# Moved SBUF homes, attention results stored as two parts, and another order of loads in a one-core encoder layer

## The chip, the core and the metric

The kernel runs on one core of one Trainium2 chip. The metric is device time in microseconds, the median of several runs of the same program; lower is better. The engines named here are PE (TensorE, matrix products), PEld (its weight loads), DVE (VectorE), ACT (ScalarE), POOL (GpSimd) and SP (SyncE, whose queue issues nearly all DMA transfers). SBUF is the on-chip memory of 128 partitions; PSUM holds the results of the matmuls. An address below is a byte offset within a partition.

## The reference

One layer over a sequence of 2048 tokens of width 1024, in float32. Two sub-layers follow each other; both take a normalised input that is scaled and shifted by values worked out from a conditioning vector c.

```
mod = silu(c) @ w_ada + b_ada                  # six vectors: shift, scale, gate, twice
h = rmsnorm(x, g1) * (1 + sc1) + sh1
q, k, v (two groups of 8 heads of 64) = split(h @ w_in)
o_sb = stick_breaking_attention(q_sb, k_sb, v_sb)              # strictly causal
o_ca = chunked_relpos_attention(rmsnorm(q_ca), rmsnorm(k_ca), v_ca, rel_bias)
x = x + gt1 * (concat(o_sb, o_ca) @ w_o)
h = rmsnorm(x, g2) * (1 + sc2) + sh2
x = x + gt2 * (square(relu(h @ w1)) @ w2)
```

Stick-breaking attention weighs key s for query t by sigmoid(z_ts) times the product of the (1 - sigmoid) of all keys between them. The other group is a softmax over the query's chunk of 64 and the eight chunks before it, with a learned bias for the distance.

## The kernel before

The host hands the sequence over reversed and transposed, so that tokens lie along the free dimension. They are cut into four blocks of TB = 512 (numbered g or tb, 0 to 3) and the width into KT = 8 slices of P = 128.

**Two parts for every operand.** A float32 matrix product is made as three fast products: each operand is split into a high part (rounded by a copy on ACT, L128) and a low part (the rest, by a subtraction on DVE or POOL, L129), and `mm3` (L186 onwards) adds high*high, high*low and low*high into one PSUM bank. A part tile has the shape [128, 2, 512]: high, then low, 4096 bytes a partition. In a matmul one operand is loaded first and stays (the weights, PEld) and the other is streamed past it (the moving operand).

**Three stages.** The first projects h onto q, k and v (tiles pq, pt) and also prepares w_o, stored to DRAM as parts in `scr_wo`, and the bias. Some of the projections of blocks 1 and 0 are left to the second stage. The second stage is the attention: for every head and block there are units (SB for the first group, CA for the second) of four steps each, 448 steps in all. A step makes scores (z, cz, ct), weights (sigmoid and a scan on DVE, or a softmax), and, eight steps later, transposes of the weights (wt, against the constant ident), their two parts (wth, wtl) and the products with the values (acc). Instructions of PE, ACT, DVE and POOL stand in program order here; SP's order is made by a scheduler at build time, with eight transfers in flight at most by its semaphores. Loads of q, k and v are issued two units ahead.

**Filler.** Between the steps PE gets other matmuls, a few at a time, from a list of generators: `fill_qkv` for block 1 (its moving operand ht1 is still in SBUF), `fill_qkv` for block 0 (moving operand fht, one load of 4 MB from `scr_h`), and `outproj(g)` for g = 3, 2, 1, the output projection of an attended block. `fill` hands out credit per step, so that the list ends about with the attention; after certain yields it rests for some steps (RESTS). What is left at the end is run by `drain`, and `outproj(1)` is: its rows 4 to 7 stand behind the last acc.

**Results of the attention.** `finish` puts the two halves of a head together on ACT and DVE; behind every second head, the [128, 512] float32 tile goes to `scr_m` (L592), 32 in all. `outproj` (L822) loads the eight of its block again as mo, and splits them into the tile mx on ACT and POOL, two before its first row and the rest within it. mx, fht and ht1 share one home, the pool hxp, of one buffer of 32 KB.

**Behind the attention** comes the third stage, in one list of steps. Eight steps `Mixed(0, n)` project block 0 (tile pso): step 0 loads and splits the eight tiles of scr_m (L1284 to L1286), and each step's w_o parts (wo) and row of x (xr) are loaded one step ahead, from L1290 on. `right_blocks(1, k)` (tiles ty, h), four calls at steps 2 to 5, load four tiles each of scr_x, scale them by POOL and ACT, combine and split them on DVE and ACT into the operands h of the MLP. The MLP makes its two products by a scheme of seven products in place of eight (Strassen's, in Winograd's form): `First` (ps<-h,opw, w1) and `Second` (ps<-oph,opv, w2), each for two halves mb of the sequence, 1344 matmuls a time.

A pool is a stretch of SBUF that is cut into a fixed number of equal buffers; pools are stacked, and a pool opened only to fill space (padn, pado, padp, padm) moves what is stacked on it. Homes in this program: h at 8192 + 4096 i, opw, oph and opv at 155456 + 4096 i, ident at 1152. The stack begins with 1024 bytes reserved for DMA descriptors.

Of the kernel before, what the change touches and what calls it, by code (L numbers as in the profile page):

```python
# [18 lines left out]
P = 128  # L19
# [3 lines left out]
NH = 8  # L23
# [44 lines left out]
def encoder_kernel(ctx, tc, xT, c, g1, g2, w_in, gqk, bias, w_o, w1, w2, w_ada, b_ada, out):  # L68
# [11 lines left out]
    hxp = hx.enter_context(tc.tile_pool(name="hxp", bufs=1))  # L80
# [7 lines left out]
    scr_m = scratch("scr_m", [P, TB], NTB, KT)  # L88
# [89 lines left out]
    def norm_apply(which, x, k, dst, pl, tg):  # L178

        j = 3 * which * KT + k  # L180
        a, b = aff[:, which, k : k + 1], mod[:, j : j + 1]
        hi, lo = dst[:, k, 0, :], dst[:, k, 1, :]
        act.activation(x, x, AF.Identity, scale=a, bias=b)
        split(hi, lo, x)
# [37 lines left out]
    with ExitStack() as ph:  # L222
# [3 lines left out]
        np_ = ph.enter_context(tc.tile_pool(name="np_", bufs=2))  # L226
        stp = ph.enter_context(tc.tile_pool(name="stp", bufs=4))
# [46 lines left out]
        def project(piece, tb, ht, wh, wl):  # L274
# [4 lines left out]
            if not ca and kind < 2:  # L279
                for n in range(2):  # L280
                    ps = pp.tile([P, TB], F32, tag="ps", name=f"pq{nm}_{n}")
                    cl = slice(n * P, (n + 1) * P)
                    for k in range(KT):
                        mm3(ps, wh[:, k, cl], wl[:, k, cl], ht[:, k, 0, :], ht[:, k, 1, :], k == 0, k == KT - 1)
# [5 lines left out]
            for t2 in range(2):  # L290
                ps = pp.tile([P, TB], F32, tag="ps", name=f"pt{nm}_{t2}")
                for tt in range(2):
                    tl = slice((2 * t2 + tt) * P, (2 * t2 + tt + 1) * P)
                    for k in range(KT):
                        mm3(
                            ps[:, tt * CW : (tt + 1) * CW], ht[:, k, 0, tl], ht[:, k, 1, tl],
# [96 lines left out]

        def h_tile(tb):
            if tb % 2:
                return hxp.tile([P, KT, 2, TB], F32R, tag="hx", name=f"ht{tb}")
            return hp.tile([P, KT, 2, TB], F32R, tag="hp", name=f"ht{tb}")
# [52 lines left out]
        for k in range(KT):  # L450
# [11 lines left out]
            for m, p in enumerate(first):  # L462
                hi, lo = (wh2[:, k], wl2[:, k]) if p == 2 else (wide[:, k, 0, p], wide[:, k, 1, p])
                for n in range(2):
                    cl = slice(n * P, (n + 1) * P)
                    mm3(
                        pss[2 * m + n], hi[:, cl], lo[:, cl], hts[3][:, k, 0, :], hts[3][:, k, 1, :],
# [29 lines left out]
        for n, (f, p, t) in enumerate(jobs):  # L497
# [18 lines left out]
            if (f, p, t) == (1, 6, 1):  # L516
                norms.flush()
                end_norm(0, h_tile(0))
                sp.dma_start(scr_h, hts[0].bitcast(F32))
# [16 lines left out]
    with ExitStack() as ph:  # L536
        kp0 = ph.enter_context(tc.tile_pool(name="kp0", bufs=3))
        owp = ph.enter_context(tc.tile_pool(name="owp", bufs=3))
        fp = ph.enter_context(tc.tile_pool(name="fp", bufs=3))
# [3 lines left out]
        pado.tile([P, 304], F32, tag="pad", name="pado")  # L543
        zw = ph.enter_context(tc.tile_pool(name="zw", bufs=12))
        wtp = ph.enter_context(tc.tile_pool(name="wtp", bufs=4))
        padp = ph.enter_context(tc.tile_pool(name="padp", bufs=1))
        zp = ph.enter_context(tc.tile_pool(name="zp", bufs=6))
        padp.tile([P, 656], F32, tag="pad", name="padp")
# [33 lines left out]
        def finish(u):  # L582
# [8 lines left out]
            if u.h % 2:  # L591
                sp.dma_start(scr_m[u.g, u.ca * 4 + u.h // 2], o)  # L592
# [182 lines left out]
        RESTS = {"pause": 3, "wait": 4, "next": 1, "start": 3}  # L775

        def fill_qkv(tb, ht, pieces):

            if ht is None:
                ht = hxp.tile([P, KT, 2, TB], F32R, tag="hx", name=f"fht{tb}")  # L780
                sp.dma_start(ht.bitcast(F32), scr_h)
# [8 lines left out]
            for n, piece in enumerate(pieces):  # L790
                grp, hf = divmod(piece, 2)
                w, nxt = nxt, []
                for j in range(2):
                    nm = f"f{tb}_{piece}_{j}"
                    ps = ppd.tile([P, TB], F32, tag="ps", name=f"p{nm}")
                    last = 0 if grp < 2 else 1
                    for tt in range(last + 1):
                        tl = slice((2 * j + tt) * P, (2 * j + tt + 1) * P)
                        for k in range(KT):
# [3 lines left out]
                            for i, (a, b) in enumerate(((0, 0), (0, 1), (1, 0))):  # L803
                                flags = {"start": k == 0 and i == 0, "stop": k == KT - 1 and i == 2}
                                if grp < 2:
                                    pe.matmul(ps, wk[:, a, j * P : (j + 1) * P], ht[:, k, b, :], **flags)
                                    yield 1.0
                                else:
                                    pe.matmul(ps[:, tt * CW : (tt + 1) * CW], ht[:, k, b, tl], wk[:, a, :], **flags)
# [12 lines left out]
        def outproj(g):  # L822
            mx = hxp.tile([P, KT, 2, TB], F32R, tag="hx", name=f"mx{g}")
            mo = {}

            def fetch(k):
                mo[k] = fp.tile([P, TB], F32, tag="xs", name=f"mo{g}_{k}", bufs=KT)
                sp.dma_start(mo[k], scr_m[g, k])

            def load(n):  # L830
                w = owp.tile([P, 2, KT, P], F32R, tag="ow", name=f"ow{g}_{n}")
                sp.dma_start(w.bitcast(F32), scr_wo[n,])
                return w, load_residual(g, n, fp)

            def part(k):
                split(mx[:, k, 0, :], mx[:, k, 1, :], mo[k], pool)

            for k in range(KT):
                fetch(k)
            nxt = load(0)  # L840
            yield "pause"
            part(0)
            yield "next"
            part(1)
            yield "next"
            for n in range(KT):
                w, xr = nxt
                if n + 1 < KT:
                    nxt = load(n + 1)
                ps = ppd.tile([P, TB], F32, tag="ps", name=f"po{g}_{n}")  # L850
# [530 lines left out]
```

## Time and profile before

| | |
|---|---|
| median of 3 runs | 2763.18 us (2763.0 to 2770.11) |
| the profiled execution | 2766.69 us, its span 2764.9 us |
| busy share of the span | PE 96%, PEld 81%, DVE 71%, ACT 55%, POOL 38% |
| granted TensorE clock, mean | 0.984 |
| DMA | 636.75 MB, mean 230 GB/s |

The stages in the span: projections to about 452 us, attention and filler to about 1420, the rest of outproj(1) to 1438, Mixed to 1507, First(1) to about 1820, Second(1) to about 2140, First(0) to about 2450, Second(0) to the end.

In the views, a group reads: line, engine, operation, out<-in, partitions x elements, count, busy time, mean duration of one in ns, and the idle time of the engine before them with what ended it. Since matmuls are pipelined, a matmul's duration is longer than the distance from its start to the next one's. A wait reads: who waited, for whom, how long in total, how often, the longest. A window reads: stretch, length, busy time and count of each engine, then the granted clock, the share of the DMA engines and their rate.

### The profile page before, as it was taken

The page shows a single profiled execution, that of the slowest core. Times are in us where ns is not written, and L with a number is a line of the kernel's source. Part 1 is how long each engine was busy: PE and PEld are TensorE (multiplying, and loading weights), DVE is VectorE, ACT ScalarE, POOL GpSimd, SP SyncE. Part 2 cuts the span into 40 slices and gives each one's busy share as a digit, 9 for nine tenths or more (in the row PEclk, how much of TensorE's full clock was granted, in tenths as well). Part 3 has the DMA queues.
Part 4 walks back from the last instruction along what each step waited for, and adds up shares of the span by engine and source line. Part 5 has one row for each costly group of instructions (what it writes and reads, how often), then busy time and mean ns, then how long its engine had stood idle before and what let it go on. Part 6 is the DMA issues. An engine that isn't in the chain of part 4 may idle for free.

```text
span 2764.9 us, 42993 instructions
## 1 busy us (share of the span) xinstructions
PE 2651.2 (96%) x14192; PEld 2238.1 (81%) x14192; DVE 1955.3 (71%) x3333; ACT 1534.3 (55%) x2926; POOL 1050.4 (38%) x1112
## 2 busy tenths in 40 slices
PE   6998999899999999999897999999999999999999
PEld 5898998778778987778775888888878888888887
DVE  7565575789789878889757787765587666655564
ACT  5422433778688778878644444454455454544443
POOL 5342454456456666777524333200022423200000
PEclk9999999999999999999998999999999999999999
DMA  8978886878887687555666777785576444465574
GB/s 316 333 277 308 300 285 208 255 240 237 276 253 234 200 237 229 178 179 176 183 220 235 254 264 251 267 298 211 187 260 232 155 147 146 165 202 189 194 258 172
DMA packets 310190, 636.75 MB, mean 230 GB/s; under 512 B 29264, under 2 KB 118352, under 8 KB 300752
## 3 DMA queue, kind: packets, MB, share of 16 engines
q1 hardware_dynamic: 309328, 632.44, 68.9%
q8 instruction: 112, 1.84, 0.3%
q10 hardware_dynamic: 640, 1.57, 0.2%
q14 instruction: 110, 0.90, 0.1%
HBM read 450.92 MB, written 182.98 MB: 229 GB/s over the span
## 4 chain that ended last, share of the span: by engine, by line
PE 79%; DVE 6%; DMA 6%; issue 3%; ACT 3%; POOL 2%; SPq 1%; DVEq 0%; ACTq 0%; POOLq 0%
PE ps L42 43%; PE acc L42 6%; PE wt L42 5%; PE pt L42 5%; PE pf L42 5%; PE z L42 5%; PE po L42 4%; PE pq L42 3%; PE cz L42 1%; DMA ty<-scr_x 1%; DMA wa<-in_w_ada_dram 1%; DVE p L42 1%; DMA k<-scr_k 1%; POOL cy L133 1%; DVE h L129 1%
## 5 line engine op out<-in xcount | busy, mean ns | idle before, releaser
L42 PE MATMUL ps<-h,opw 128*128 128x512 f32 x2688 | 630.3, 396 | 4.2 <-ACT opw L128 2.5
L42 PE MATMUL ps<-oph,opv 128*128 128x512 f32 x2688 | 614.2, 390 | 5.3 <-DVE oph L129 3.5
L42 PEld LDWEIGHTS ps<-h,opw 128*128 128x128 f32 x2688 | 505.2, 188 | 129.2 <-ACT opw L128 2.9
L42 PEld LDWEIGHTS ps<-oph,opv 128*128 128x128 f32 x2688 | 505.3, 188 | 112.3 <-DVE oph L129 4.6
L42 POOL TENSOR_TENSOR b<-b,p 128x512 f32<-128x512 f32 (+1 forms) x320 | 361.2, 1129 | 209.2 <-DVE p L42 189.4
L42 DVE TENSOR_TENSOR wtl<-wt,wth 128x512 fp32r<-128x512 f32 (+3 forms) x544 | 290.8, 546 | 55.5 <-ACT wth L42 53.3
L42 ACT CAST wth<-wt 128x512 fp32r<-128x512 f32 (+3 forms) x544 | 258.0, 484 | 126.7 <-PE wt L42 110.4
L42 PE MATMUL pt<-wh,ht 128*128 128x256 f32 x1664 | 308.1, 286 | 6.6 <-DVE ht L129 4.4
L128 ACT CAST oph<-hr 128x512 fp32r<-128x512 f32 x224 | 139.3, 622 | 286.0 <-PE ps L42 275.3
L129 DVE TENSOR_TENSOR oph<-hr,oph 128x512 fp32r<-128x512 f32 x224 | 156.7, 700 | 197.3 <-ACT oph L128 197.1
L42 PEld LDWEIGHTS pt<-wh,ht 128*128 128x128 f32 x1664 | 262.6, 193 | 8.6 <-DVE ht L129 5.7
L42 DVE TENSOR_TENSOR_SCAN p<-z,p,zero 128x512 f32<-128x512 f32 x192 | 246.2, 1282 | 31.9 <-ACT z L42 28.5
L42 PE MATMUL pt<-wl,ht 128*128 128x256 f32 x832 | 236.9, 285 | 0.0
L42 PE MATMUL acc<-wth,v 128*128 128x512 f32 (+3 forms) x544 | 222.6, 413 | 1.4 <-DMA v<-scr_v 1.4
L42 ACT ACTIVATE b<-z 128x512 f32<-128x512 f32 (+1 forms) x320 | 171.6, 536 | 64.5 <-PE z L42 45.9
L42 POOL TENSOR_TENSOR e<-e,cols 128x640 f32<-128x640 f32 (+4 forms) x128 | 143.4, 1123 | 155.7 <-DVE cols L42 102.1
L42 PE MATMUL z<-k,q 128*128 128x512 f32 (+3 forms) x640 | 187.4, 375 | 11.5 <-DVE st L198 5.3
L1033 POOL TENSOR_TENSOR ts<-w 128x512 f32<-128x512 f32 x32 | 45.2, 1414 | 378.3 <-DMA w<-in_w_dram 331.3
L42 PE MATMUL acc<-wtl,v 128*128 128x512 f32 (+3 forms) x544 | 186.6, 350 | 0.0
L42 PE MATMUL wt<-ident,b 128*128 128x128 f32 x1088 | 173.7, 275 | 4.6 <-DVE cols L42 3.2
L42 PE MATMUL po<-mx,ow 128*128 128x512 f32 x576 | 165.6, 402 | 11.9 <-POOL mx L42 7.7
L129 DVE TENSOR_TENSOR opw<-ts,opw 128x512 fp32r<-128x512 f32 x128 | 117.4, 920 | 79.6 <-ACT opw L128 79.1
(210 smaller groups left out, 4742.6 us busy)
## 6 DMA issues: line engine op xcount, KB each, us to landing
hr<-scr_hid SPq DMA_DIRECT2D x112, 512.0 KB, 3.5
v<-scr_v SPq DMA_DIRECT2D x136, 256.0 KB, 4.2
k<-scr_k SPq DMA_DIRECT2D x268, 128.0 KB, 4.2
w<-in_w_dram SPq DMA_DIRECT2D x64, 512.0 KB, 4.1
wr<-scr_s SPq DMA_DIRECT2D x64, 512.0 KB, 4.3
q<-scr_q SPq DMA_DIRECT2D x124, 256.0 KB, 5.2
fw<-scr_w SPq DMA_DIRECT2D x28, 1024.0 KB, 7.3
wa<-in_w_ada_dram SPq DMA_DIRECT2D x48, 512.0 KB, 6.5
```

What stands on the lines that cost most here:

```text
L42: return lambda *x, **y: self.tc.keep_in_program_order(f(*x, **y))
L128: act.copy(hi, src)
L129: (lo_eng or dve).tensor_tensor(lo, src, hi.bitcast(F32), op=ALU.subtract)
L133: pool.tensor_tensor(y, v, mhalf[:, :n], op=ALU.pow)
L1033: eng.tensor_tensor(out, a, b, op=op)
```

## The change

No arithmetic is changed. There are four parts.

1. *Homes.* The reserved stretch falls from 1024 to 256 bytes, pads are added, changed and removed, and pools are stacked in another order. Every operand pair of the three-product scheme now has equal addresses modulo 256 in the built program. ident is at 384, and the transposed weights and qh are 128 apart from it modulo 256; they were equal.
2. *Parts.* A new job `keep`, one step behind `finish`, splits the pair of heads (ACT and POOL) into a tile os (one buffer) and stores both parts, 512 KB, into an enlarged `scr_m`. outproj and Mixed load parts and split nothing. The filler outproj(g) is appended by the last `keep` of its block.
3. *Slices.* hxp has eight buffers of 4 KB and a new pool hx2 has four. A class `Filler` loads moving operands slice by slice, four at a time, in turn into hx2 and the two halves of hxp; the first four are loaded in the last piece of the filler before ("ahead"), the rest when it begins.
4. *Order behind the attention.* Raw buffers go from 4 to 8; w_o parts are loaded for four steps at the start, then three steps ahead; rows of x apart from them, one step ahead; right_blocks(1, k) come at steps 0 to 3 instead of 2 to 5; First's w1 tiles are fetched at the last step but one of Mixed.

```diff
-    hxp = hx.enter_context(tc.tile_pool(name="hxp", bufs=1))
+    hxp = hx.enter_context(tc.tile_pool(name="hxp", bufs=KT))
...
-    scr_m = scratch("scr_m", [P, TB], NTB, KT)
+    scr_m = scratch("scr_m", [P, 2, TB], NTB, KT)
...
+        padn = ph.enter_context(tc.tile_pool(name="padn", bufs=1))
+        padn.tile([P, 32], F32, tag="pad", name="padn")
...
         def h_tile(tb):
             if tb % 2:
-                return hxp.tile([P, KT, 2, TB], F32R, tag="hx", name=f"ht{tb}")
-            return hp.tile([P, KT, 2, TB], F32R, tag="hp", name=f"ht{tb}")
+                return [hxp.tile([P, 2, TB], F32R, tag="hx", name=f"ht{tb}_{k}") for k in range(KT)]
+            whole[tb] = hp.tile([P, KT, 2, TB], F32R, tag="hp", name=f"ht{tb}")
+            return [whole[tb][:, k] for k in range(KT)]
...
+        hx2 = ph.enter_context(tc.tile_pool(name="hx2", bufs=KT // 2))
+        xrp = ph.enter_context(tc.tile_pool(name="xrp", bufs=3))
...
-        pado.tile([P, 304], F32, tag="pad", name="pado")
+        pado.tile([P, 80], F32, tag="pad", name="pado")
...
-        padp = ph.enter_context(tc.tile_pool(name="padp", bufs=1))
         zp = ph.enter_context(tc.tile_pool(name="zp", bufs=6))
-        padp.tile([P, 656], F32, tag="pad", name="padp")
...
             if u.h % 2:
-                sp.dma_start(scr_m[u.g, u.ca * 4 + u.h // 2], o)
+                soon.append(lambda: keep(u, o))
+
+        def keep(u, o):
+
+            os = op.tile([P, 2, TB], F32R, tag="os", name=f"os{u.nm}", bufs=1)
+            split(os[:, 0, :], os[:, 1, :], o, pool)
+            sp.dma_start(scr_m[u.g, u.ca * 4 + u.h // 2], os.bitcast(F32))
+            if u.ca and u.h == NH - 1 and u.g > 0:
+                filler.append(Filler(outproj, u.g))
...
-        RESTS = {"pause": 3, "wait": 4, "next": 1, "start": 3}
+        RESTS = {"wait": 4, "start": 3}
+        turn = [0]
+
+        class Filler:
+            def __init__(self, make, *x):
+                self.tiles = []
+                self.gen = make(self, *x)
+                self.src = next(self.gen)
+
+            def fetch(self, n):
+                while len(self.tiles) < n:
+                    pl = (hx2, hxp, hxp)[turn[0] % 3]
+                    turn[0] += 1
+                    for k in range(len(self.tiles), len(self.tiles) + KT // 2):
+                        t = pl.tile([P, 2, TB], F32R, tag="hx", name=f"fx{turn[0]}_{k}")
+                        sp.dma_start(t.bitcast(F32), self.src(k))
+                        self.tiles.append(t)
...
-        def outproj(g):
-            mx = hxp.tile([P, KT, 2, TB], F32R, tag="hx", name=f"mx{g}")
...
-            for k in range(KT):
-                fetch(k)
+        def outproj(self, g):
+            yield lambda k: scr_m[g, k]
...
+            mx = self.moving()
             nxt = load(0)
-            yield "pause"
-            part(0)
-            yield "next"
-            part(1)
-            yield "next"
+            yield "wait"
             for n in range(KT):
                 w, xr = nxt
                 if n + 1 < KT:
                     nxt = load(n + 1)
+                else:
+                    yield "ahead"
...
+        accp = ph.enter_context(tc.tile_pool(name="accp", bufs=12))
         padm = ph.enter_context(tc.tile_pool(name="padm", bufs=1))
-        padm.tile([P, 4000], F32, tag="pad", name="padm")
+        padm.tile([P, 80], F32, tag="pad", name="padm")
+        rawp = ph.enter_context(tc.tile_pool(name="rawp", bufs=8))
         opp = ph.enter_context(tc.tile_pool(name="opp", bufs=8))
-        rawp = ph.enter_context(tc.tile_pool(name="rawp", bufs=4))
-        accp = ph.enter_context(tc.tile_pool(name="accp", bufs=12))
...
                     for k in range(KT):
-                        m = kept(f"m{g}_{k}")
-                        sp.dma_start(m, scr_m[g, k])
-                        Mixed.parts[k] = operand(m, f"m{g}_{k}", dve if k % 2 else pool)
+                        m = Mixed.parts[k] = opp.tile([P, 2, TB], F32R, tag="op", name=f"opm{g}_{k}")
+                        sp.dma_start(m.bitcast(F32), scr_m[g, k])
...
-            at(2 + k, lambda k=k: right_blocks(1, k))
+            at(k, lambda k=k: right_blocks(1, k))
...
-            for m in (n, n + 1) if n == 0 else (n + 1,):
-                if m < len(steps) and isinstance(steps[m], Mixed):
+            for m in range(KT // 2) if n == 0 else (n + 3,):
+                if m < KT:
                     steps[m].load()
+            for m in (0, 1) if n == 0 else (n + 1,):
+                if m < KT:
+                    steps[m].load_row()
+            if n == KT - 2:
+                steps[KT].fetch()
...
-    nc = _bacc.Bacc("TRN2", target_bir_lowering=False, num_devices=1, dynamic_dma_scratch_size=1024)
+    nc = _bacc.Bacc("TRN2", target_bir_lowering=False, num_devices=1, dynamic_dma_scratch_size=256)
```

## The prediction

> **What bounds the kernel now.** I read the page from the top: busy time by engine, the 40 slices, the chain of waits. Then two stretches by window, the groups by shape, who waits for whom, and the order of time where the waits sit.
>
> ```profile
> PE 2651.2 (96%) x14192; PEld 2238.1 (81%) x14192; DVE 1955.3 (71%) x3333; ACT 1534.3 (55%) x2926; POOL 1050.4 (38%) x1112
> ...
> PEclk9999999999999999999998999999999999999999
> ...
> PE 79%; DVE 6%; DMA 6%; issue 3%; ACT 3%; POOL 2%; SPq 1%; DVEq 0%; ACTq 0%; POOLq 0%
> ```
>
> TensorE is the bound: 96% busy and 79% of the chain. Time is won where its matmuls follow closer on each other, or where it stands still. For the first, the groups by shape, and the windows of the MLP's matmuls (busy us, count, clock, DMA share, GB/s):
>
> ```profile
> L42 PE MATMUL ps<-h,opw 128*128 128x512 f32 x2688 | 630.3, 396 | 4.2 <-ACT opw L128 2.5 <-DVE opw L129 1.7
> L42 PE MATMUL ps<-oph,opv 128*128 128x512 f32 x2688 | 614.2, 390 | 5.3 <-DVE oph L129 3.5 <-DVE opv L129 1.3 <-ACT opv L128 0.3
> ```
>
> ```profile
> 1550.00:1800.00 250.00, 250.00 (x1073) 1.00 0.76 262
> 2150.00:2400.00 250.00, 250.00 (x1074) 1.00 0.44 147
> 2460.00:2560.00 100.00, 100.00 (x443) 1.00 0.57 199
> 2560.00:2760.00 200.00, 200.00 (x884) 1.00 0.59 207
> ```
>
> The two halves of the MLP issue the same 2688 matmuls of one shape at full clock without a pause, but the first (h, opw) needs 250/1073 = 233 ns for each and the second (oph, opv) 300/1327 = 226 ns. The built program's addresses show a difference: h lies at remainder 0 of 256 bytes and opw at 64; oph and opv both at 64. Other rows agree, start to start in the trace: pq with both at 128 takes 227.0 ns, pq with ht at 0 and its weights at 128 takes 232.3; po with both at 0, in the unbroken run before 1438 us, 226.7. So neither zero nor the stage separates them; equal remainders do.
>
> For the standing still, who waited, and three stretches of windows:
>
> ```profile
> PE pso L42 <- DMA wo<-scr_wo: 13.7, 6, 7.0
> ...
> PE po L42 <- POOL mx L42: 7.7, 4, 4.9
> ```
>
> ```profile
> 1171.00:1191.00 20.00, 13.13 (x63) 9.60 (x63) 10.21 (x19) 10.18 (x21) 16.05 (x18) 0.74 0.47 132
> 1191.00:1211.00 20.00, 20.00 (x112) 16.79 (x111) 17.41 (x22) 15.84 (x33) 14.52 (x23) 1.00 0.57 178
> 1321.00:1341.00 20.00, 15.00 (x73) 12.15 (x72) 10.20 (x40) 10.53 (x22) 17.12 (x15) 0.83 0.49 133
> 1345.00:1365.00 20.00, 19.14 (x122) 16.66 (x121) 15.02 (x50) 12.73 (x30) 8.79 (x7) 1.00 0.75 204
> 1438.00:1510.00 72.00, 52.43 (x197) 39.77 (x195) 43.47 (x53) 29.16 (x47) 28.00 (x20) 0.89 0.74 249
> ```
>
> The columns of the windows are PE, PEld, DVE, ACT, POOL, clock, DMA share, GB/s. Where outproj(2) and outproj(1) begin, TensorE issues 63 and 73 instructions in 20 us instead of 112 and 122, with POOL busier than it and a granted clock of 0.74 and 0.83. From 1438 to 1510 us lies Mixed: 192 matmuls that need 43.5 us at 226.7 ns.
>
> **The change part by part.** The sum is made against the profiled execution, 2766.7 us (span 2764.9 and 1.8 around it), which stands 3.5 above the median of the runs shown, 2763.2.
>
> *A, homes.* In the changed program every pair of fp32r operands has one remainder, 0 of 256. First MLP half: 2688 x (232.9 - 226.1) = -18.3. Its operands stay covered: DVE is busy 248 of 320 us there, which would be 82% of the shorter stretch. Second half, z, po, pf: equal before and after, 0. pq: 192 matmuls, -1.0. pt: 1344 of its 256-column matmuls become equal; start to start the trace has 118.7 ns unequal and 120.0 equal, so +1.7. acc: 1088 become equal; if the 560 of 512 columns gained the full 6.8 ns it is -3.8, but equal z and unequal acc, both mixed into the attention, run at 230 to 232 ns alike, which is 0; I take -1, nearer to the row of that stage. Transposes (wt, px, 1776) lose their equality, ident being at 128. At 128 columns the mean is 276 ns equal (ct) and 278 unequal (acc<-wtl), so up to +3.6; the pt rows give -2.3; I take +1, nearer to the rows of the same width. Sum -17.6, ends -24 and -13.
>
> The Trainium skill ("TensorE: Matmul & The Clock Gate", section "Step-by-step: what each phase is for") says that the array has two independent read ports into SBUF, so that loading the next weights takes no read bandwidth from the running matmul. By that rule A is 0 and the sum 2741 instead of 2723. The 233 and 226 above speak against it.
>
> *B, outproj inside the attention.* It goes: 24 loads of 256 KB and 24 splits in bursts of eight (ACT 0.62 us, POOL 1.29 us each) ahead of the first po row. Those are the stalls: 20 - 20 x 63/112 = 8.8 us and 20 - 20 x 73/122 = 8.0; the 4 MB load of fht shows 2.1 us of TensorE waiting. Together -18.9. It comes: 32 splits, one behind every second head, each with a 512 KB store. In the attention that is 8 more of each (ACT 5.0, POOL 10.3 us), on engines 83% (ACT) and 74% (POOL) busy from 1200 to 1300 us, while DVE, the fullest at 92%, gets none. If none shows it is 0; if the 32 ACT parts lie on the path, 32 x 0.62 = +20. I take +4, near to none, since the weights that POOL and ACT prepare are used eight steps later. Each store waits on SP for POOL; behind it stand loads of q, k and v, which are issued two units ahead. The moving slices come as 512 KB loads, half of them in the last piece of the job before; the weights (1 MB, 7.3 us to land) still come behind them, under a rest of four steps of 2.2 us (448 steps in 990 us). Bytes: +16.8 MB, 56 us at the 300 GB/s of the first slices, over 990 us whose DMA share is 0.44 to 0.84: hidden; with a full queue it would be a rival. Phase 1 with ht in slices and the smaller scratch issue the same work: 0, hidden in any case by TensorE's own 160 of 160 us there. Sum -15, ends -20 and +2.
>
> *C, behind the attention.* Mixed takes from 1438.2 to the first ps at 1507.2, and 2.1 us more stand in its first step: 71 us for 43.5, so 27.6 could go. It goes: 8 splits, and weights that arrive one step ahead. It comes: opm 8 x 512 KB instead of 256, four steps of weights at once (4.2 MB), rows and right_blocks behind them. What is late next: the order on SP. In the built program the last opm and all wo loads stand behind the store of row 7 of outproj(1), which waits for the last po. Before, the first wo half was issued at 1432.3, the second at 1436.5; that store went out at 1440.3, so wo now goes at 1441 and lands some 5 us later: pso starts about 5 us later than its 1440.4. Then weights are there for four steps. But right_blocks' ty loads stand behind 4.7 MB (16 us at 300 GB/s), and its 44 DVE operations (7 splits and 4 sums a block at 0.7, 34 us, some with POOL beside them) go from about 1463 to 1500; the last ty loads, which wait on SP for DVE to free a buffer, hold wo 6 and wo 7 up for some us. First then starts at about 1502 instead of 1510: -8. Ends: -20 (three quarters of the 27.6) and +5 (the later start alone). w1 is fetched two steps earlier, under that.
>
> *The rest of the MLP.* Raw buffers go from 4 to 8; TensorE waits for no raw load there before, so 0. The 8 us of DVE waits at 2027 to 2045 stay.
>
> Sum: -17.6 - 15 - 8 = -40.6, so 2726.1 for such an execution and 2722.6, say 2723, as a median.
>
> **The rivals.**
> - *Only the homes pay.* The waits of B and C change their name: po waits for its weights behind the slices, right_blocks sets First's start as before. For it: in Mixed, POOL waited 37.1 us for ty, TensorE only 13.7 for wo. Against it: the outproj stalls are named POOL and ACT, and that work leaves. 2763.2 - 17.6 = 2746.
> - *The homes don't pay.* The two MLP halves also differ in who wrote the operands and when. For it: z is equal and still takes 232. Against: pq has both speeds in one stage. Then B and C alone: 2763.2 - 23 = 2740.
> - *Slower: the spread splits hold SP.* The store of each pair waits for ACT, then POOL; SP issues in order, so the loads of k and v behind it start late, and TensorE waits at z, cz and acc (DMA k and v cost it 7.8 us now). It cancels the gain at 40.6/32 = 1.3 us a store; at 2 us each, 64 us, the time is 2787. Against it: the loads run two units, about 17 us, ahead.
> - *Nothing shows*: DMA, now fuller behind the attention, gives back what the homes win; about 2763.
>
> **How the numbers follow.** Forecast 0.66, only homes 0.16, homes don't pay 0.09, slower 0.05, nothing 0.04. About 0.3% (8 us) is what a measurement of this kernel can tell from no change. Faster is the first three, 0.91. The forecast's own range takes the three ends as independent: below, the square root of 6.4, 5 and 12 squared, 15; above, of 4.6, 17 and 13 squared, 22; so 2708 to 2745. The range takes in the two smaller gains above, 2750, and below 6 us of the quarter of C's 27.6 that its good end leaves out, 2702.
>
> **What would show it.** A: ps<-h,opw at 390 ns, and 250 us of it holding 1105 matmuls; if it stays at 1073, the homes were not the cause. B: no po waiting for POOL or ACT mx, no 20 us with a clock of 0.74; new waits of po for ow or fx would say the first rival, of z and acc for k and v the third. C: pso starting near 1446 on the old scale, waits for wo below 8 us, the first ps some 8 us closer. Wrong it would be if a home in the running program differs from the built one, or if DVE, at 92% in the widest part of the attention, sets its pace once TensorE no longer stalls.

## The result and the profile after

The changed kernel takes 2738.24 us (median of five, 2737.44 to 2746.92) against 2763.18 for the kernel before in the same session: ratio 0.9914, 95% interval 0.9893 to 0.9935. It is faster, and by 25 us instead of the 40 forecast. The profiled execution took 2737.44 us, its span 2735.7.

The page of the changed kernel: busy time by engine and the granted clock in 40 slices.

```profile
PE 2625.1 (96%) x14192; PEld 2235.5 (82%) x14192; DVE 1929.8 (71%) x3329; ACT 1528.5 (56%) x2926; POOL 1023.8 (37%) x1116
...
PEclk9999999999999999999998999999999999999999
```

The groups by shape, and the windows of the MLP's matmuls (stretch, length, then busy us and count of PE, PEld, DVE, ACT, POOL, the clock, the DMA share, GB/s):

```profile
L42 PE MATMUL ps<-oph,opv 128*128 128x512 f32 x2688 | 614.9, 391 | 4.1 <-DVE opv L129 3.5 <-DVE oph L129 0.6
L42 PE MATMUL ps<-h,opw 128*128 128x512 f32 x2688 | 613.4, 391 | 6.7 <-ACT opw L128 4.0 <-DVE opw L129 2.7
```

```profile
1540.00:1790.00 250.00, 250.00 (x1104) 207.02 (x1103) 199.15 (x265) 125.08 (x214) 66.16 (x48) 1.00 0.79 274
2120.00:2370.00 250.00, 250.00 (x1105) 207.01 (x1104) 145.60 (x212) 124.35 (x210) 78.46 (x59) 1.00 0.45 152
...
```

The two halves of the MLP now run alike: 391 ns each, and 1104 and 1105 matmuls in 250 us where there had been 1073 and 1074. The waits of TensorE, and the windows at the start of outproj(2) and outproj(1) and behind the attention:

```profile
PE pso L42 <- DMA wo<-scr_wo: 15.9, 3, 9.9
...
PE pf L42 <- DMA fw<-scr_w: 4.5, 2, 2.9
...
PE acc L42 <- DMA v<-scr_v: 3.1, 1, 3.1
```

```profile
1171.00:1191.00 20.00, 17.87 (x112) 15.10 (x111) 15.48 (x27) 12.04 (x24) 11.55 (x20) 1.00 0.74 222
...
1321.00:1341.00 20.00, 18.55 (x115) 16.11 (x115) 15.50 (x55) 12.93 (x29) 10.20 (x9) 1.00 0.43 118
...
1425.00:1498.00 73.00, 50.64 (x196) 39.41 (x194) 48.94 (x54) 31.16 (x50) 30.64 (x20) 0.86 0.77 274
```

No po waits for POOL or ACT any more, and the two stretches of 20 us hold 112 and 115 matmuls instead of 63 and 73, at full clock. Behind the attention nothing is won: the first ps starts 69.3 us after the last po, where it had been 69.0, and the wait for wo has grown from 13.7 to 15.9.

The change by stages, from the starts of the same matmuls in both profiled executions (us):

| stretch | before | after | difference |
|---|---|---|---|
| start to the first z | 460.9 | 457.2 | -3.7 |
| first z to the last matmul of outproj(1) (attention) | 977.3 | 967.8 | -9.5 |
| from there to the 15th step of First (the seam) | 112.7 | 113.9 | +1.2 |
| from there to the end | 1214.0 | 1196.8 | -17.2 |

The first row is mostly scatter: in the twelve further executions below the first z starts between 456.4 and 459.3, among them 458.4 in the kernel before with one pad changed. The seam is measured to the 15th step of First (of 112 steps of 12 matmuls in each half) because a start of First that is a few us sooner can be lost again in its first steps. The other rows of such tables below are read in the same way.

### The profile page after: what moved, and what is told of

Its sections match the earlier page's. It is cut to its first block, busy times and chain, and to the rows that moved or that the text cites. A ratio compares the mean times of both kernels' runs of the same rounds, so it can differ in the third digit from the quotient of the medians.

```text
span 2735.7 us, 42897 instructions
## 1 busy us (share of the span) xinstructions
PE 2625.1 (96%) x14192; PEld 2235.5 (82%) x14192; DVE 1929.8 (71%) x3329; ACT 1528.5 (56%) x2926; POOL 1023.8 (37%) x1116
## 3 DMA queue, kind: packets, MB, share of 16 engines
q1 hardware_dynamic: 310336, 649.22, 70.7%
## 4 chain that ended last, share of the span: by engine, by line
PE 52%; DVE 2%; DMA 1%; ACT 1%; issue 1%; POOL 0%; SPq 0%; DVEq 0%; ACTq 0%
PE ps L42 44%; PE po L42 3%; PE acc L42 2%; PE wt L42 2%; PE z L42 1%; DVE h L129 1%; DVE ty L1063 1%; PE cz L42 0%; DMA wo<-scr_wo 0%; DMA ty<-scr_x 0%; DMA out_dram<-tx 0%; DVE tx L1301 0%; DVE p L42 0%; POOL ty L1106 0%; ACT ty L1107 0%
## 5 line engine op out<-in xcount | busy, mean ns | idle before, releaser
L42 PE MATMUL ps<-h,opw 128*128 128x512 f32 x2688 | 613.4, 391 | 6.7 <-ACT opw L128 4.0
L42 PEld LDWEIGHTS ps<-oph,opv 128*128 128x128 f32 x2688 | 506.4, 189 | 110.8 <-DVE opv L129 4.2
L42 ACT ACTIVATE z<-z 128x512 f32<-128x512 f32 (+1 forms) x320 | 170.6, 533 | 0.0
L42 PEld LDWEIGHTS wt<-ident,b 128*128 128x128 f32 x1088 | 133.9, 141 | 37.5 <-DVE cols L42 6.9
L42 PE MATMUL po<-fx,ow 128*128 128x512 f32 x576 | 162.5, 397 | 0.0
```

The source lines that it names most:

```text
L42: return lambda *x, **y: self.tc.keep_in_program_order(f(*x, **y))
```

## The experiments

Three questions: are the homes the cause in the MLP, as the prediction had it, or one of its rivals; what does the attention lose again; why is nothing won at the seam.

### Homes alone

```diff
-        padm.tile([P, 4000], F32, tag="pad", name="padm")
+        padm.tile([P, 3984], F32, tag="pad", name="padm")
```

This is the kernel before, with opw and all that lies behind the pad 64 bytes lower.

> The kernel before with one pad 16 floats shorter (4000 to 3984), so that in the third stage opw and h have equal addresses modulo 256 (their difference is 256 modulo 512) and every other pair stays as equal as it was; nothing else changes. Theory of the homes, remainder of 256: each of the 2688 matmuls of First follows 6.5 to 6.8 ns sooner, so 17.5 to 18.3 us less, ratio 0.9935 +- 0.001 (2745 to 2746), ps<-h,opw at 390 ns a matmul instead of 396. Rival 1, the two halves differ in who wrote the operands and when: ratio 1.000, ps<-h,opw stays at 396. Rival 2, it is the remainder of 512 that matters: 1.000 too.

Measured: 2743.05 us (2742.69 to 2747.41), ratio 0.9935, interval 0.9914 to 0.9956. The groups by shape of this kernel:

```profile
L42 PE MATMUL ps<-oph,opv 128*128 128x512 f32 x2688 | 614.0, 390 | 3.6 <-DVE oph L129 1.9 <-DVE opv L129 1.3 <-ACT opv L128 0.3
L42 PE MATMUL ps<-h,opw 128*128 128x512 f32 x2688 | 612.3, 390 | 4.3 <-ACT opw L128 2.5 <-DVE opw L129 1.8
```

The 630.3 us of ps<-h,opw became 612.3 by moving a pad, with the same instructions and the same writers. So it is the homes, and a difference of 256 bytes modulo 512, which h and opw have here, does no harm: the remainder of 256 counts. This is the larger part of the whole change in one number.

### How unequal is unequal

The kernel after, with the eight buffers of the pool opp 4128 bytes apart:

```diff
+        def moved(nm):
+            t = opp.tile([P, 2 * TB + 8], F32R, tag="op", name=nm)
+            return t[:, 0 : 2 * TB].rearrange("p (l t) -> p l t", l=2)
...
-        padm.tile([P, 80], F32, tag="pad", name="padm")
+        padm.tile([P, 16], F32, tag="pad", name="padm")
...
-            o = opp.tile([P, 2, TB], F32R, tag="op", name=f"op{nm}") if dst is None else dst
+            o = moved(f"op{nm}") if dst is None else dst
```

> The kernel after, with the eight operand buffers of the third stage 4128 bytes apart instead of 4096, so that the weights opw stand at 0, 32, 64 ... 224 from h modulo 256 in turn, and oph and opv always at unequal remainders. One run, matmuls read apart by their difference. Theory of the homes as a step (equal or not): difference 0 stays at 226 to 227 ns, each other at 233; First +15 us, Second +18, so 2771. Rival, a graded effect: 32 and 224 stand between 226.5 and 233, 128 highest; 2755 to 2768. Rival, not the homes: no difference between the groups, 2738.

Measured: 2770.86 us in one run. The groups by shape:

```profile
L42 PE MATMUL ps<-oph,opv 128*128 128x512 f32 x2688 | 630.9, 396 | 3.3 <-DVE opv L129 3.2
L42 PE MATMUL ps<-h,opw 128*128 128x512 f32 x2688 | 625.5, 394 | 2.1 <-DVE cx L1067 1.0 <-DVE opw L129 1.0
```

The matmuls ps<-h,opw read apart by (home of the next weights - home of the moving operand) modulo 256, mean distance from start to start:

| difference, bytes | 0 | 32 | 64 | 96 | 128 | 160 | 192 | 224 |
|---|---|---|---|---|---|---|---|---|
| ns | 228.7 | 232.9 | 233.4 | 234.1 | 232.8 | 233.6 | 229.0 | 233.2 |

The smallest step tried, 32 bytes, already costs all of it; it is a step, not a slope. Two columns are not as the first theory has them: 192 stands out at 229.0, and 0 itself stays 2 ns above the 226.7 of the kernel after; why is open in both. The eight give a mean of 232.2, so First pays 2688 x (232.2 - 226.7) = 14.8 us; Second, whose pairs all stand 224 apart, has 233.4 and pays 2688 x (233.4 - 226.8) = 17.7. Together 32.5, and the one run is 2770.86 - 2738.24 = 32.6 us longer. That the two agree so closely is luck: in the traces 29.8 us of it lie behind the 15th step of First, and the attention, where nothing was changed, happens to be 4.2 longer.

### The spread splits

```diff
-            os = op.tile([P, 2, TB], F32R, tag="os", name=f"os{u.nm}", bufs=1)
-            split(os[:, 0, :], os[:, 1, :], o, pool)
-            sp.dma_start(scr_m[u.g, u.ca * 4 + u.h // 2], os.bitcast(F32))
+            for l in range(2):
+                sp.dma_start(scr_m[u.g, u.ca * 4 + u.h // 2][:, l, :], o)
```

> The kernel after without the 32 splits of the attention results: the whole float32 pair of heads is stored into both halves of scr_m, so the bytes stored and loaded are the same and what is left out is 32 copies on ACT and 32 subtractions on POOL and the waits for them (the output's projection then counts the results twice). Theory 1, the spread splits are what the attention lost (it drifted 7.3 us against before up to the second outproj): 4 to 7 us less, 2731 to 2734. Theory 2, the drift comes from new waits for weights and more bytes: at most 1 us less, 2737 to 2738.

Measured: 2734.27 us (2730.72 to 2736.01), ratio 0.9894, interval 0.9871 to 0.9916. The attention takes 966.1 us; eight executions of kernels that share the attention of the changed one take 967.2 to 972.0, mean 969.1. So the 32 splits cost some 3 us there, 4 by the medians, 0.3 us short of the first theory's range. It is weak evidence: the one execution is 1.1 us under the lowest of the eight, and the intervals of this kernel and of the changed one overlap.

### Weights ahead of the slices

In `fill_qkv` and in `outproj` the first weights are loaded before `self.moving()`:

```diff
-            mx = self.moving()
             nxt = load(0)
+            mx = self.moving()
```

> The kernel after with one order changed: the first weights of a filler (fw, ow) are loaded ahead of the second half of its moving slices instead of behind it. Theory 1, the new waits of pf for fw (4.5 us in three) come from the weights standing behind the slices: they go, 3 to 4 us less, 2734 to 2735. Theory 2, the transfers only change places and pf or po waits for the slices fx instead: 0, 2738 +- 1.

Measured: 2732.52 us (2731.09 to 2736.73), ratio 0.9892, interval 0.9869 to 0.9914. TensorE's waits for weights, of this kernel:

```profile
PE acc L42 <- DMA v<-scr_v: 1.5, 1, 1.5
...
PE pf L42 <- DMA fw<-scr_w: 0.2, 1, 0.2
```

The wait for fw falls from 4.5 to 0.2 us, no wait for slices comes in its place, and the wait for v halves. The attention takes 964.8, and 965.6 and 959.1 in the two later kernels with the same edit. The waits go as the first theory has it: the weights stood behind the slices on SP. The time falls by 5.7 us, more than its range, though the intervals overlap. The gain lies ahead of outproj(3): from the first z to its first po, 556.4 and 558.2 us with the old attention, 557.2 to 562.1 in the eight with the changed one, and 554.8, 557.1 and 549.0 in the three with the weights first; behind that point the three take 408.4 to 410.1, the eight 406.9 to 410.0. That it lies at the start of one filler is not shown: from the first z to the first pf of block 0 the eight take 244.3 to 249.1 and the three 240.9, 245.5 and 239.0, so one of them is no shorter.

### Four orders behind the attention

First, the wo loads moved to ACT's queue:

```diff
-                    sp.dma_start(w[l].bitcast(F32), scr_wo[n,][:, l, :, :])
+                    act.dma_start(w[l].bitcast(F32), scr_wo[n,][:, l, :, :])
```

> The kernel after with the loads of wo behind the attention issued from ACT's queue instead of SP's, where they stood behind the store of the last row of outproj(1). Theory 1, the start of First is set by the chain of right_blocks on DVE (busy from 1449 to 1499 us with hardly a gap), not by wo: pso starts up to 9 us sooner, but the first ps comes within 2 us of where it was, 2736 to 2738. Theory 2, the late wo sets it: first ps up to 9 us sooner, 2729 to 2731.

Second, right_blocks ahead of all:

```diff
-            at(k, lambda k=k: right_blocks(1, k))
+            at(k - 1, lambda k=k: right_blocks(1, k))
...
+        for job in jobs.pop(-1):
+            job()
```

> The kernel after with right_blocks(1, 0) put ahead of everything else of the third stage, and the other three one step earlier each, so that the first ty loads stand on SP ahead of opm and wo. Theory 1, the DVE chain sets First's start: it begins some 10 us sooner, while DVE is idle, and the first ps comes 5 to 10 us sooner, 2728 to 2733. Theory 2, wo sets it: wo comes later still, first ps no sooner or some us later, 2738 to 2742.

Third, both edits:

> Both edits together: wo on ACT's queue and right_blocks(1, 0) first. Theory 1 (DVE chain alone): as with right_blocks first, 2728 to 2733. Theory 2 (wo alone): as with wo on ACT's queue, 2729 to 2731. If both are limits in turn, only this one gains the whole, 8 to 14 us: 2724 to 2730.

Fourth, the old order with everything else kept:

```diff
-            at(k, lambda k=k: right_blocks(1, k))
+            at(2 + k, lambda k=k: right_blocks(1, k))
...
-            for m in range(KT // 2) if n == 0 else (n + 3,):
+            for m in (0, 1) if n == 0 else (n + 1,):
...
-            if n == KT - 2:
-                steps[KT].fetch()
```

> The kernel after with the order of loads behind the attention undone: right_blocks at steps 2 to 5, wo one step ahead, no early fetch of w1; parts, slices, homes and the eight raw buffers stay. Theory 1, the new order behind the attention is worth nothing (the stretch takes 72.8 us, before 71.9): 2737 to 2741. Theory 2, the new order is worth the 8 us of the forecast and something else lost as much: 2745 to 2748. Theory 3, the new order costs, since eight wo loads stand ahead of ty: 2730 to 2735.

Measured, with the kernels of the next three sections (us; "start" is the last po to the first pso, then TensorE's waits by their reason, then the seam of the table of stages):

| kernel | start | for wo | for opm or ty | of ps for opw or cx | seam | median |
|---|---|---|---|---|---|---|
| before | 2.2 | 13.7 | 0 | 4.2 | 112.7 | 2763.18 |
| after | 10.3 | 15.9 | 0 | 6.7 | 113.9 | 2738.24 |
| wo on ACT's queue | 1.3 | 10.2 | 5.2 | 0.9 | 110.5 | 2736.89 |
| right_blocks first | 11.7 | 2.5 | 11.3 | 6.8 | 112.0 | 2737.86 |
| both | 3.2 | 9.7 | 8.6 | 1.1 | 114.7 | 2737.47 |
| old order | 7.9 | 18.8 | 0 | 4.0 | 117.9 | 2740.98 |
| wo on two queues | 1.3 | 10.1 | 5.4 | 3.4 | 110.8 | 2732.76 |
| fewer low parts | 10.5 | 16.1 | 0 | 4.4 | 111.4 | 2734.84 |
| scaling on DVE | 10.2 | 12.2 | 0 | 12.6 | 113.9 | 2740.39 |
| ty without wait | 1.3 | 1.8 | 5.3 | 11.7 | 110.8 | 2729.56 |

The start is in part the same time as the waits beside it. With wo on ACT's queue pso starts nine us sooner and First does not: the last wo loads then come late, behind ACT's own work. With right_blocks first the first ps comes 64.8 us after the last po instead of 69.3, and most of it is lost in the next steps, 2.9 us of it to a wait for cx. The first came out as its first theory has it. The second misses the range of its second theory by 0.1 us, with a first ps nearly as early as the first theory has it. The third is in none of its ranges: the gain expected from lifting two limits did not come. (Ratios to the kernel before: 0.9906, 0.9891 to 0.9921; 0.9915, 0.9900 to 0.9930; 0.9908, 0.9891 to 0.9924; and 0.9925, 0.9910 to 0.9940 for the old order.) The old order takes 4 us more in the seam and 2.7 by the medians, at the upper end of its first theory. By these, one execution each and medians whose intervals overlap, the new order is worth some 3 us against the old one, and the rest of the change has made this stretch dearer by as much or more.

### Wo on two queues

With the weights ahead of the slices, wo for the first four steps goes on ACT's queue and for the last four on SP:

```diff
-                    sp.dma_start(w[l].bitcast(F32), scr_wo[n,][:, l, :, :])
+                    (act if n < KT // 2 else sp).dma_start(w[l].bitcast(F32), scr_wo[n,][:, l, :, :])
```

> The kernel after with weights loaded ahead of the moving slices, and behind the attention the loads of wo for the first four steps issued from ACT's queue, those for the last four from SP as in the kernel after; with all eight on ACT's queue the last three came late. Theory 1, wo and the ty loads behind it both hold First up: pso starts some 7 us sooner, ty follows, first ps 3 to 6 us sooner than with the weights' order alone (2732.5), 2726 to 2730. Theory 2, the DVE work of right_blocks sets First's start whatever the loads do: 2731 to 2734.

Measured: 2732.76 us (2726.83 to 2737.0), ratio 0.9891, interval 0.9871 to 0.9911; the median is that of the weights' order alone, in the second theory's range, but of its four runs two lie in the first theory's range and two some 8 us higher. In the trace pso starts nine us sooner behind the last po than with the weights' order alone and the first ps 3.7 us sooner (67.0 us after the last po instead of 70.7), which is the first theory's size; in the seam 2.3 us of it are left (110.8 instead of 113.1). So this run does not decide between the two.

### Is it the DVE chain

Two edits in right_blocks. For h 5, 6 and 7 the low part is a copy on ACT instead of a subtraction on DVE:

```diff
-                operand(src, "", dst=hops[i, k])
+                if plain:
+                    for l in range(2):
+                        act.copy(hops[i, k][:, l, :], src)
+                else:
+                    operand(src, "", dst=hops[i, k])
```

> The kernel after with 12 of the 28 low parts of h in the first right_blocks left out (for h 5, 6 and 7 both parts are copies on ACT, so First computes something else): DVE does 12 of its 44 operations there less, 12 us at the mean of 1.0 us, ACT 12 copies of 0.62 us more. Theory 1, the chain on DVE sets First's start and, through the ty buffers, the last wo loads: first ps 6 to 10 us sooner, 2728 to 2732. Theory 2, the loads set it: at most 2 us, 2736 to 2738.

And POOL's multiplication is put on DVE:

```diff
-                pool.tensor_tensor(t, t, rows[tb], op=ALU.mult)
+                (dve if mb else pool).tensor_tensor(t, t, rows[tb], op=ALU.mult)
```

> The kernel after with the 16 multiplications by rows in the first right_blocks moved from POOL (1.55 us each) to DVE. In the trace DVE operations with two SBUF inputs take 0.68 us alone and 1.6 us while POOL multiplies, so DVE would have 60 x 0.68 = 41 us instead of 43.7 for 44. Theory 1, it is POOL beside it that stretches the chain: no loss, 0 to 5 us sooner, 2733 to 2738. Theory 2, DVE pays for its own operations at full length: 16 x 0.68 = 11 us later, 2745 to 2749.

Measured: 2734.84 us (2731.97 to 2739.9), ratio 0.9902, interval 0.9886 to 0.9918, with a quarter of DVE's operations gone; and 2740.39 us (2737.1 to 2745.02), ratio 0.9923, interval 0.9906 to 0.994, with 16 operations more on it. Neither is in the range of either theory. In the seam the first wins 2.5 us. The second loses nothing there, 113.9 as before, though DVE has a third more instructions in the chain: all 16 products and 24 of the 28 low parts have no POOL beside them and take 0.68 us each. The first ps even comes 60.6 us after the last po instead of 69.3; one wait of this kernel takes that back:

```profile
PE ps L42 <- DVE opw L129: 12.6, 1, 12.6
```

The low part of First's first weights stands behind the whole chain on DVE, so even where Mixed ends sooner, First waits. The median is 2.2 us above that of the kernel after, but the intervals overlap, so no loss is shown.

### SP without its waits for ty

To the kernel with two queues one edit is added; accp's twelve buffers are mostly free there:

```diff
-                t = y[nm] = temp(f"y{mb}_{k}_{nm}")
+                t = y[nm] = (kept if mb and kk >= HK else temp)(f"y{mb}_{k}_{nm}")
```

> The kernel with weights ahead of the slices and wo for the first four steps on ACT's queue (2732.8), and in addition two of the four loads of every first right_blocks go to the twelve buffers of accp, which are mostly free there, so that SP no longer waits for DVE to free ty buffers and the last wo loads come sooner; the work on every engine is the same. Theory 1, SP's waits for DVE, which hold the last wo loads up, set First's start: TensorE's waits for wo fall from 10.1 us to under 5, first ps 4 to 7 us sooner, 2726 to 2729. Theory 2, several limits stand almost level behind the attention (TensorE's gaps from 1415 to 1545 us summed to 19 to 26 us in each of the nine orders read so): the wait for wo goes and a wait for DVE (opw, cx) comes, first ps at most 2 us sooner, 2731 to 2734.

Measured: 2729.56 us (2727.19 to 2730.89), ratio 0.9891, interval 0.9874 to 0.9907: the lowest median of all, below the range of the second theory and just above that of the first. The trace decides by the waits. TensorE from 1415 to 1540 us, with two queues:

```profile
PE pso L42 <- DMA wo<-scr_wo: 10.1, 4, 5.6
...
PE ps L42 <- DVE opw L129: 2.1, 1, 2.1
PE ps L42 <- DVE cx L1063: 1.3, 1, 1.3
```

and with ty without wait:

```profile
PE ps L42 <- ACT opw L128: 8.4, 1, 8.4
...
PE ps L42 <- DVE cx L1063: 1.9, 1, 1.9
PE pso L42 <- DMA wo<-scr_wo: 1.8, 3, 0.9
PE ps L42 <- DVE opw L129: 1.4, 1, 1.4
```

The wait for wo goes from 10.1 to 1.8 and a wait for opw of 8.4 comes; the seam is 110.8 in both. That is the second theory in kind: one wait went, another came. In size it is neither: the new wait is named ACT where the theory has DVE, and the first ps, 67.0 us after the last po with two queues and 64.4 here, came 2.6 sooner instead of at most 2, which the steps behind it gave back. The lower time of this profiled execution arose in the attention, 959.1 us against 965.6 with the same program there, so it is scatter between executions as far as these runs can tell; it is the lowest of its four runs, and the profiled one with two queues the highest. This kernel and the one with two queues are both faster than the kernel before; that they are faster than the changed kernel (0.9914, up to 0.9935) the intervals leave open.

## Why the prediction was right or wrong

**A, homes, -17.6: right, the term and the cause.** From the 15th step of First to the end 17.2 us went; of these, 16.8 in the two First stages alone (starts of the same matmuls, 587.5 us before and 570.7 after, and 570.7 with homes alone), which makes 17.9 with the 168 matmuls ahead of that step at 6.8 ns each. The kernel with homes alone won 19.1 by the medians, with an interval from 12 to 24. The row of 1105 matmuls in 250 us that was asked for reads 1104 and 1105. Of the small terms, pq came: the 192 that became equal follow each other after 227.5 ns instead of 232.5, -1.0 us. So did the loss of pt, a row of 256 columns where unequal is the faster: 119.9 ns instead of 118.8, +1.5 us. Acc did not gain (means of 477 and 395 ns before, 476 and 396 after), and the transposes did not lose (wt 275 and 278 before, 274 and 277 after). Together about -17.4. The rival that the homes do not pay is out. The Trainium skill ("TensorE: Matmul & The Clock Gate", section "Step-by-step: what each phase is for") has it that loading the next weights takes no read bandwidth from the running matmul. The 233 and 227 ns of two programs that differ in one pad speak against it for these float32r matmuls of 512 columns, as long as the remainders differ; what in the chip makes it so no run here shows.

**B, attention, -15: the direction right, the size too large.** With all executions of the two attentions together, 977.3 and 979.4 against a mean of 969.1, it won 9.3 us. Two terms of the sum failed. The stalls were put at 18.9, 16.8 of it at outproj(2) and outproj(1), 8.8 and 8.0; from the first po of outproj(3) to the end of outproj(1) the time fell from 421.0 and 421.2 to a mean of 409.4, so 12 us. Counted from first po to first po, 4.2 us of it came with outproj(2) and 4.1 with outproj(1), half of what was put there, and 3.4 with outproj(3), where nothing was. The step at fault is that the matmuls missing from a window were taken as time that comes back in full; already the waits that the trace of the kernel before names there come to less, 11.8 us:

```profile
PE po L42 <- POOL mx L42: 7.7, 4, 4.9
...
PE po L42 <- ACT mx L42: 4.1, 1, 4.1
```

The windows did fill; part of it came back between them. DVE is busy 131.6 of 145 us from 1165 to 1310 in the kernel after, which was named as the thing that could make it wrong; that it is the cause was not tried. The other is that the weights "still come behind them", the slices, "under a rest of four steps", costed at nothing: ahead of outproj(3), where the load of fht was to save 2.1 us, 2.4 were lost (557.3 us before, 559.7 after, means; 555.9 without the spread splits), and in the three runs with the weights first and nothing else changed there the attention was 4.3, 3.5 and 10 us shorter, most of it in that stretch. The spread splits, taken at +4, cost 3 to 4 as far as one execution and overlapping intervals can say.

**C, behind the attention, -8: wrong.** The gain did not come. The seam was 111.6 (112.7 less the 1.1 us that the homes save in its first 14 steps) and 108.1 in the two executions of the kernel before and of homes alone, and is 113.9, 111.2 and 113.1 in the three with the new order: a mean of 2.9 lost, between -0.4 and +5.8. (The kernel with buffers 32 apart, a fourth, has 111.7, some 0.9 of it by its homes.) The step that failed is "First then starts at about 1502 instead of 1510". Two sizes in it were off. pso was to start 5 us late; it started 10.3 us behind the last po instead of 2.2, so 8 late. The larger one is the chain of right_blocks. It was to run from 25 to 62 us behind the last po and ran from 25 to 71, on time at its start and nearly ten us late at its end. It was taken as 44 operations of 0.7 us, 34 us (31 by that product; three were for POOL). The groups of DVE from 1425 to 1500 us in the kernel after:

```profile
L129 DVE TENSOR_TENSOR h<-ty,h 128x512 fp32r<-128x512 f32 x28 | 26.9, 998 | 1.6 <-ACT h L128 1.0 <-DMA wo<-scr_wo 0.5
L1063 DVE TENSOR_TENSOR ty<-ty,ty 128x512 f32<-128x512 f32 x16 | 16.8, 1053 | 0.3
L211 DVE SCALAR_TENSOR_TENSOR cxr<-pso,mod,cxr 128x512 f32<-128x512 f32 x8 | 5.9, 743 | 21.7 <-DMA ty<-scr_x 18.4 <-PE pso L42 3.3
```

They take 43.7 us, and 49.6 with the eight residuals between them that the prediction left out. The chain of work that ended last, the same kernel from 1420 to 1500 us (start, length, what), shows where the time goes:

```profile
1428.58 10.23 DMA wo<-scr_wo
1438.83 7.14 DMA ty<-scr_x
1445.97 5.04 POOL ty L1106 x4
...
1465.80 1.70 DVE ty L1063
1467.50 1.71 DVE h L129
1469.21 1.71 DVE ty L1063
...
1497.15 1.03 DVE opw L129
1498.23 2.07 PE ps L42 x4
```

First the loads, wo and then ty behind it; then POOL, ACT and DVE in turn to the end. The experiments add that this is not one limit but several that stand almost level: wo's start, SP behind DVE, DVE's chain and the first opw behind that chain. Most edits moved the wait that they aimed at, and in nine orders the seam stayed between 110.5 and 117.9 us. The first rival's sentence on C, "right_blocks sets First's start as before", came nearest; its B did not hold, since po waited for no weights (pf did, for fw) and the attention won 9 us. Whether lifting all of them at once would win more, with the first ty loaded while DVE stands idle (6.6 of 40 us busy from 1400 to 1440), is open.

The sum as measured: -17.4 - 9.3 + 2.9 = -23.8, beside 24.9 between the medians. The median alone could not have told which account is right: 2738 lies 15 us above the forecast, inside its range, and within 2 us of the 2740 of a rival that the traces rule out, the one in which the homes don't pay. No case of SP being held by the stores showed: the waits of acc, cz and z for v and k are 3.1, 4.7 and 1.0 us, 8.8 together where they had been 7.8.

## What to carry to other kernels

Where operands are streamed past weights that are reloaded all the time, compare the SBUF addresses of the two, modulo 256 here, as one compares shapes: two groups of equal matmuls with different distances from start to start are the sign, and a pad is the price. That holds for the matmuls of 512 columns here; at 256 columns equal remainders cost 1 ns. A wait that is removed is worth what the next limit behind it allows; where three or four of them stand within a few us, count the distance between two fixed matmuls on either side and not the waits. And a load put behind a larger one on the same queue is not hidden by that alone: here 4.5 us of it came on TensorE.

## What the runs showed of the hardware

A DVE operation on two SBUF operands is slowed by a POOL operation beside it. The order of time in the kernel after, DVE and then POOL (start, length; the three of POOL follow without a gap):

```profile
1465.72 1.78 DVE L1063 TENSOR_TENSOR ty<-ty,ty 128x512 f32<-128x512 f32 x1
1467.43 1.78 DVE L129 TENSOR_TENSOR h<-ty,h 128x512 fp32r<-128x512 f32 x1
1469.13 1.78 DVE L1063 TENSOR_TENSOR ty<-ty,ty 128x512 f32<-128x512 f32 x1
1470.84 0.68 DVE L129 TENSOR_TENSOR h<-ty,h 128x512 fp32r<-128x512 f32 x1
```

```profile
1465.54 4.82 POOL L1106 TENSOR_TENSOR ty<-ty,r 128x512 f32<-128x512 f32 x3 [4.42 <-DMA ty<-scr_x]
```

From 1425 to 1500 us the 23 such operations with no POOL beside them take 0.68 us, the nine wholly beside POOL 1.63. The residual, whose first operand lies in PSUM, takes 0.74 either way. With POOL's products moved to DVE nearly all take 0.68, so it is POOL and not the data. POOL pays too: its first product behind the attention takes 1.29 us with DVE idle, and the second and third of the three above 1.74. The Trainium skill ("SBUF — State Buffer", section "SBUF: two separate sides") says that DVE with two SBUF inputs and GpSimd take turns on one pair of ports, each for a whole instruction; the three operations of 1.78 us, one for each of POOL's, agree with the turns. That each turn lasts a whole instruction these rows don't show: 0.68 and 1.29 us, what the two take alone, make 1.97, and the three of DVE start 1.71 us apart. The prediction knew that POOL worked there and gave it three us; it took 13.8 (43.7 - 44 x 0.68).

Also not expected: between homes, a difference of 192 bytes costs almost nothing (229.0 ns, beside 232.8 to 234.1 for the other six unequal ones).
